# Two more block pairs of the FFN's up-projection in seven half-width products, with the sums of x they need made partly in the projection before

## The chip, the cores and the metric

The program runs on one core of a Trainium2 chip. Its time is device microseconds of one execution, and lower is better. The kernel before took 1469.0 us (median of 3 runs, 1468.36 to 1469.34).

## The reference, cut to what matters

A two-layer encoder on x of 512 tokens by 1024 channels, in float32. Each layer adds three things to x in turn: a mixer (attention in layer 0, an mLSTM in layer 1), a cross-attention to a memory of 256 tokens, and a convolutional feed-forward network (FFN). The last is what the change is about:

```
def conv_ffn(xn, w_up, conv_w, conv_b, w_down):
    h = causal_depthwise_conv(xn @ w_up, conv_w) + conv_b
    g, u = jnp.split(h, 2, axis=-1)
    return (jax.nn.gelu(g) * u) @ w_down
```

`xn` is RMS-normed x, `w_up` is 1024 by 5632, `w_down` 2816 by 1024. The cross-attention ends in a product with `wo` (1024 by 1024) that is added to x.

## The kernel before

x lies transposed in SBUF: eight blocks `x[0..7]` of 128 channels by 512 tokens. Every float32 product is made from two parts of each operand, high and low, in three matmuls (`mm3`, L290 to L292). A weight block is loaded by SP (`raw`), its high part is cast by ScalarE (`wh`), and the low part is subtracted by VectorE (`wl`, L281). So TensorE runs the products, and each operand costs the two other engines a pass.

**Up-projection by pairs.** The FFN (`ffn_steps`, from L1247) makes its 5632 hidden channels in 22 pairs: pair p is block p (gate) and block 22+p (up), 128 channels each. `plain` (from L1431) makes a pair as two blocks of eight k-steps, each step one `mm3` of 512 columns: 48 matmuls. `seven` (from L1451) makes it in Strassen's way (Winograd's form) from seven products of four k-steps with 256 columns: 84 matmuls of half the width. There the two rows of blocks of the weights are A1 and A2, each cut in two halves along k; x is cut in two halves along k and two along tokens (`HALF`). The seven products are p1, p5, p6, p2, p7, p3, p4 in the order in which they run. Products p5, p6, p7 and p4 multiply sums of quarters of x, T1, T3, T2, T4, which don't depend on the pair. These lie as high and low part in `th[k]`, `tl[k]` (k from 0 to 3, 1024 columns each).

**The forms of x.** `forms(k, at)` (L1363 to L1384) makes `th[k]`, `tl[k]`: two scalings on ScalarE into an `hs` tile (L1370), three sums on VectorE into an `sa` tile (L1374, L1381, L1382), a cast on ScalarE (L1383), and a subtraction on VectorE. It takes block k of x for the one half along k and block k+4 for the other. All four forms are made in the FFN, two behind pair 0 and two behind pair 1.

**Which pairs are which.** `SEVEN` names pairs 4 to 21; pairs 0 to 3 are plain.

**Weights of a seven pair.** SP loads both halves of A into `sa` (L1280), then a DMA issued by POOL adds A2 on top of it (`onto`, L1460, with accumulation); SP also loads A1 (`raw`) and half of A2 (`ra`). VectorE makes two more sums (`sb`, L1480, L1486). Then there are five splits into high and low part. Three `sa` tiles, two `sb`, one `ra`, and one each of the small split tiles `s2`, `a22`, `s4`; the wide split tiles `wh`, `wl` have three each and are shared with the plain blocks.

**Between products.** p6 and p7 collect in one PSUM bank, Y. VectorE reads it (`c22`, L1520) before p4 may write it; p3 runs between. VectorE also makes `c12` (L1520) and scales the pair by the norm (L1543). The rest, `tail`, is 4 taps of the convolution on VectorE (L1404), one multiply (L1414), one cast and one subtraction (`al`). Two `hs` tiles hold the unfinished pairs.

**Fill.** From pair 5 on, `fill()` puts blocks of the down-projection (12 matmuls of 512 columns each, `down`) at two places in a pair: between c22 and p3, and behind p4. There are 8 blocks for each group of four activations, so pairs 5 to 16 and 18 have two each, pair 19 has one (ahead of p3), and pairs 4, 17, 20 and 21 none.

**What sets the order.** In the mixers and in the cross-attention a planner, `Plan`, takes the items in the order of their priorities as soon as its own estimate says they are ready; in the FFN another, `Sched`, gives each engine at each step the task that can start first, the one due first among those that can start at once. Each engine then runs its queue in order. A tile that lies where an earlier stage's tile lay waits for that tile's last reader (`reuse_waits="tile"`).

**The stage before the FFN.** `xattn` (L1122) holds its keys in `kth`, `ktl` and its values in `vh`, `vl`, 32 KB a partition in all. Its last part, `p_out` (blocks m = 0 to 7, priorities 100 to 107), is the projection with `wo`: per block 24 matmuls of 512 columns, then on VectorE the sum to x (L618), on ScalarE the scaled high part `xh` (L602), on VectorE the low part `xl` (L603), and the squares for the next norm (L593 to L597). The keys, the values and the scores are done by then.

Of the kernel before, what the change touches and what calls it, by code (L numbers as in the profile page):

```python
# [1 line left out]

# [7 lines left out]
F32 = mybir.dt.float32  # L10
# [15 lines left out]
SEVEN = (4, 5, 6, 7, 8, 9, 10, 11, 12, 13, 14, 15, 16, 17, 18, 19, 20, 21)  # L26
# [209 lines left out]
class Builder:  # L236
# [885 lines left out]
    def xattn(self, layer):  # L1122
        nc, t, tc = self.nc, self.t, self.tc
        with tc.tile_pool(name=f"xa{layer}", bufs=1, reuse_waits="tile") as mp:
            self.mp = mp
            pl = Plan(self.plan, [st["banks"][0] for st in self.fills], s=2, w=2, e=4, q=2, pt=2, wt=3)
            self.pad(mp, 192)
            kth = mp.tile([P, KB8, MEM], F32R, name=f"kth{layer}")
            ktl = mp.tile([P, KB8, MEM], F32R, name=f"ktl{layer}")
            self.pad(mp, 64)  # L1130
            vh = mp.tile([P, 2, DM], F32R, name=f"xvh{layer}")
            vl = mp.tile([P, 2, DM], F32R, name=f"xvl{layer}")
# [4 lines left out]
            for h in range(4):  # L1137
                p = 10 + 10 * h
                ke = []
                for m in (2 * h, 2 * h + 1):  # L1140

                    def keys(ps, m=m, at=0):
                        tmp = self.til(mp, "tmp")
                        nc.vector.tensor_tensor(out=tmp[:, :MEM], in0=ps[:, at : at + MEM], in1=self.memrb, op=ALU.mult)
                        self.split(kth[:, m, :], ktl[:, m, :], tmp[:, :MEM])
# [32 lines left out]
                if h % 2 == 0:  # L1178
                    cs = slice(256 * h, 256 * h + 512)

                    def values(tk, ps, cs=cs):
                        self.evac_tok(ps, self.memr[:, tk : tk + 1], vh[:, tk, cs], vl[:, tk, cs])

                    ve = self.p_proj_tok(pl, t["xv"][layer, h // 2], self.mems, 2, values, prio=p)
# [8 lines left out]
                for i in range(4):  # L1193
# [3 lines left out]
                    def score(h=h, qs=qs, res=res, sl=sl):  # L1197
                        sp = self.bank("s")
                        for d in range(2):
                            kb = 2 * h + d  # L1200
                            self.mm3(sp[:, :MEM], qs[d][0][:, sl], qs[d][1][:, sl], kth[:, kb, :], ktl[:, kb, :], d == 0, d == 1)
# [22 lines left out]
                for d in range(2):  # L1224

                    def weigh(h=h, d=d, pts=pts):
                        c = slice(256 * h + P * d, 256 * h + P * d + P)
                        ps = self.bank("w")
                        for j in range(2):
                            self.mm3(ps[:], vh[:, j, c], vl[:, j, c], pts["h"][:, j, :], pts["l"][:, j, :], j == 0, j == 1)  # L1230
# [7 lines left out]
            self.p_out(pl, t["xo"][layer], lambda: (mh, ml), kd, "ffn", layer, None, 100)  # L1238
            pl.run()
            self.plan = pl  # L1240

# [5 lines left out]
    def ffn_steps(self, layer, mp):  # L1247
# [78 lines left out]
        own = lambda k: (self.xh[k][:], self.xl[k][:])  # L1326
# [23 lines left out]
        th, tl = ([mp.tile([P, 1024], F32R, name=f"t{i}{layer}{k}", tag=f"t{i}{k}") for k in range(4)] for i in "hl")  # L1350
# [12 lines left out]
        def forms(k, at):  # L1363

            st = {}

            def scaled(j):
                if j == 0:
                    st["t"] = hs2[st["_hs"]][:, :, 2:514]
                nc.scalar.activation(st["t"][:, j, :512], self.x[k + 4 * j][:], AF.Identity, scale=self.col("ffn", layer * 8 + k + 4 * j))  # L1370

            def first():
                st["r"] = raw_tile(st, "sa")[:]
                tt_(out=pair(st["r"][:, :512]), in0=pair(st["t"][:, 0, :512]), in1=st["t"][:, :, 256:512], op=ALU.subtract)  # L1374

            T1, T3, T2, T4 = (slice(256 * i, 256 * i + 256) for i in range(4))
            tt_ = nc.vector.tensor_tensor
            a = add("ACT", ACV, lambda: scaled(0), (), at, [("hs", st)])
            a = add("ACT", ACV, lambda: scaled(1), [a], at)
            a = add("DVE", tt(512), first, [a], at, [("sa", st)])  # L1380
            a = add("DVE", tt(256), lambda: tt_(out=st["r"][:, T2], in0=st["t"][:, 1, 256:512], in1=st["r"][:, T1], op=ALU.add), [a], at)  # L1381
            a = add("DVE", tt(256), lambda: tt_(out=st["r"][:, T4], in0=st["t"][:, 1, 0:256], in1=st["r"][:, T2], op=ALU.subtract), [a], at, (), [("hs", st)])  # L1382
            h = add("ACT", act(1024), lambda: nc.scalar.copy(th[k][:], st["r"]), [a], at)  # L1383
            formed.append(add("DVE", tt(1024), lambda: self.sub(tl[k][:], st["r"], th[k][:]), [h], at, (), [("sa", st)]))  # L1384
# [66 lines left out]
        def seven(p, fill):  # L1451
# [46 lines left out]
            X = lambda h, l: (lambda k: (self.xh, self.xl)[0][k + 4 * h][:, HALF[l]], lambda k: self.xl[k + 4 * h][:, HALF[l]])  # L1498
# [75 lines left out]
        for p in range(22):  # L1574
# [5 lines left out]
            if p < 2:  # L1580
                for k in (2 * p, 2 * p + 1):
                    forms(k, clock[0] + 4.0 * (k % 2))
# [247 lines left out]
    def finish(self, mp, ah, al):  # L1830
# [7 lines left out]
        outs = [self.til(mp, f"t{i}{k}", (P, 1024), F32R, bufs=1).bitcast(F32)[:, :512] for k in range(4) for i in "hl"]  # L1838
# [64 lines left out]
    def run(self):  # L1903
        tc = self.tc
        M = bass.MemoryType.PSUM
        with (
# [10 lines left out]
            for layer in range(2):  # L1917
                with tc.tile_pool(name=f"mem{layer}", bufs=1, reuse_waits="tile") as self.memp:
                    (self.mix0, self.mix1)[layer]()
                    self.xattn(layer)  # L1920
                self.ffn(layer)


def col_blocks(w):

    k, m = w.shape
    return w.reshape(k // P, P, m // P, P).transpose(2, 1, 0, 3).reshape(m // P, P, k)

# [16 lines left out]
def layout(i):  # L1945
# [23 lines left out]
    a["up"] = np.stack([col_blocks(i["ffn_w_up"][n]) for n in range(2)])  # L1969
# [40 lines left out]
```

## Time and profile before

| | |
|---|---|
| time, median of 3 | 1469.0 us |
| profiled execution: time, span | 1469.97 us, 1467.1 us |
| TensorE busy | 1452.4 us |
| VectorE busy | 1200.9 us |
| ScalarE busy | 873.7 us |
| output projection of the cross-attention, layers 0 and 1 | about 376 to 407.7 us, about 1084.5 to 1116.2 us |
| pairs 0 to 3 | 407.7 to 451.9 us, 1116.2 to 1160.4 us |

The span runs from the first to the last instruction of the profiled execution; the 2.9 us of its time beside the span are start and end. In the trace's lines a group is named by line, engine, operation and tiles: `acc<-xh,wh` is a matmul into a bank of tile `acc` from `xh` and `wh`. Two numbers ahead of a line of the timeline are its start and its duration in us. Matmuls overlap, so the distance of their starts is their price, and not their duration. Brackets hold the idle time of the engine just before and what ended it. A line of the table by stretches gives for each engine the busy time and the count, then the granted clock, the share of the DMA engines' time and GB/s. A line of the waits gives who waited for whom, the total, the times and the longest.

### The profile page before, as it was taken

The numbers are of one execution on the slowest core, as the hardware profiler recorded it, in microseconds if no ns is written. First come the engines' busy times: TensorE is split into PE (matmuls) and PEld (weight loads), VectorE is DVE, ScalarE is ACT, GpSimd is POOL, SyncE is SP. The second block draws the span as 40 slices with busy tenths as digits, with TensorE's granted clock in tenths as the row PEclk, the third lists the DMA queues.
The fourth block names the chain that finished last, engine by engine and source line by source line (L and its number), as shares of the span: only waits on it lengthen the run. The fifth ranks groups of instructions, "written<-read, shape, count | busy, mean of one in ns | idle before, by whom it ended". The sixth has DMA issues, their size and how long they took to land.

```text
span 1467.1 us, 22604 instructions
## 1 busy us (share of the span) xinstructions
PE 1452.4 (99%) x8503; PEld 1267.8 (86%) x8503; DVE 1200.9 (82%) x2136; ACT 873.7 (60%) x1533; POOL 63.3 (4%) x102
## 2 busy tenths in 40 slices
PE   9999999999999999999999999999999999999998
PEld 7888787888889999999888888888888899999987
DVE  7789985766589999999769988677557999999974
ACT  7688664544476656666457655454445766656654
POOL 0001120000001000000000100000000000000000
PEclk9999999999999999999999999999999999999999
DMA  5222333323238665652223332332323766656322
GB/s 198 87 73 73 122 117 121 115 87 114 86 130 205 168 160 158 154 159 80 85 99 109 115 101 74 121 102 100 115 87 115 187 173 165 158 160 156 109 68 77
DMA packets 64797, 179.14 MB, mean 122 GB/s; under 512 B 7072, under 2 KB 7072, under 8 KB 64688
## 3 DMA queue, kind: packets, MB, share of 16 engines
q1 hardware_dynamic: 58496, 157.71, 32.9%
q0 software_dynamic: 5184, 18.88, 7.6%
q8 instruction: 66, 1.08, 0.3%
q10 hardware_dynamic: 1008, 1.12, 0.2%
q14 instruction: 43, 0.35, 0.1%
HBM read 175.55 MB, written 2.13 MB: 121 GB/s over the span
## 4 chain that ended last, share of the span: by engine, by line
PE 80%; DVE 13%; ACT 3%; issue 2%; DMA 1%; POOL 0%; SPq 0%; ACTq 0%; DVEq 0%; POOLq 0%
PE acc L290 16%; PE acc L291 16%; PE acc L292 15%; PE w L291 5%; PE w L290 5%; PE w L292 5%; DVE wl L281 3%; PE s L290 2%; PE s L292 2%; PE s L291 2%; PE acc L351 2%; DVE c L1404 2%; PE acc L353 2%; PE acc L352 2%; DVE x L770 1%
## 5 line engine op out<-in xcount | busy, mean ns | idle before, releaser
L290 PE MATMUL acc<-xh,wh 128*128 128x512 f32 (+1 forms) x800 | 282.0, 352 | 0.1
L292 PE MATMUL acc<-xh,wl 128*128 128x512 f32 (+1 forms) x800 | 279.9, 350 | 0.2 <-DVE wl L281 0.2
L291 PE MATMUL acc<-xl,wh 128*128 128x512 f32 (+1 forms) x800 | 279.5, 349 | 0.0
L281 DVE TENSOR_TENSOR wl<-raw,wh 128x1024 fp32r<-128x1024 f32 (+4 forms) x199 | 235.7, 1186 | 27.2 <-ACT wh L284 22.8
L284 ACT CAST wh<-raw 128x1024 fp32r<-128x1024 f32 (+1 forms) x135 | 139.3, 1036 | 144.5 <-PE acc L291 88.7
L292 PEld LDWEIGHTS acc<-xh,wl 128*128 128x128 f32 x800 | 150.2, 188 | 20.8 <-DVE wl L281 0.6
L290 PEld LDWEIGHTS acc<-xh,wh 128*128 128x128 f32 x800 | 150.3, 188 | 20.4 <-ACT v L1639 0.6
L291 PEld LDWEIGHTS acc<-xl,wh 128*128 128x128 f32 x800 | 150.3, 188 | 19.9
L1404 DVE SCALAR_TENSOR_TENSOR c<-hs,vec,c 128x512 f32<-128x512 f32 x176 | 128.0, 745 | 7.6 <-ACT c L1397 6.5
L292 PE MATMUL w<-ah,wl 128*128 128x512 f32 x304 | 118.9, 391 | 0.0
L291 PE MATMUL w<-al,wh 128*128 128x512 f32 x304 | 118.5, 390 | 0.0
L290 PE MATMUL w<-ah,wh 128*128 128x512 f32 x304 | 118.4, 390 | 0.0
L1397 ACT ACTIVATE c<-hs,vec 128x512 f32<-128x512 f32 x88 | 70.7, 814 | 46.1 <-DVE hs L1543 38.0
L618 DVE TENSOR_TENSOR x<-w,x 128x512 f32<-128x512 f32 x72 | 49.5, 687 | 22.0 <-PE w L292 22.0
L292 PEld LDWEIGHTS w<-ah,wl 128*128 128x128 f32 x304 | 57.0, 188 | 12.1
L290 PEld LDWEIGHTS w<-ah,wh 128*128 128x128 f32 x304 | 57.1, 188 | 10.0
L291 PEld LDWEIGHTS w<-al,wh 128*128 128x128 f32 x304 | 57.1, 188 | 9.9
L618 DVE TENSOR_TENSOR x<-acc,x 128x512 f32<-128x512 f32 x32 | 22.0, 691 | 49.2 <-PE acc L292 49.2
L290 PE MATMUL acc<-mem,wh 128*128 128x256 f32 (+1 forms) x192 | 61.1, 318 | 0.0
L291 PE MATMUL acc<-mem,wh 128*128 128x256 f32 (+1 forms) x192 | 60.9, 317 | 0.0
L292 PE MATMUL acc<-mem,wl 128*128 128x256 f32 (+1 forms) x192 | 60.7, 316 | 0.0
L1474 ACT CAST wh<-sa 128x1024 fp32r<-128x1024 f32 x36 | 37.8, 1050 | 34.1 <-PE w L291 32.1
(470 smaller groups left out, 3985.0 us busy)
## 6 DMA issues: line engine op xcount, KB each, us to landing
raw<-in_up_dram SPq DMA_DIRECT2D x52, 512.0 KB, 3.3
sa<-in_up_dram SPq DMA_DIRECT2D x36, 512.0 KB, 3.8
sa<-in_up_dram POOLq DMA_DIRECT2D x36, 512.0 KB, 6.2
dr<-in_down_dram SPq DMA_DIRECT2D x64, 256.0 KB, 2.8
ra<-in_up_dram SPq DMA_DIRECT2D x36, 256.0 KB, 2.6
raw<-in_xk_dram SPq DMA_DIRECT2D x16, 512.0 KB, 3.4
raw<-in_wo_dram SPq DMA_DIRECT2D x16, 512.0 KB, 3.4
raw<-in_xq_dram SPq DMA_DIRECT2D x16, 512.0 KB, 3.3
```

The source lines that it names most:

```text
L281: self.nc.vector.tensor_tensor(out=lo, in0=v, in1=hi.bitcast(F32), op=ALU.subtract)
L284: self.nc.scalar.copy(hi, v)
L290: mm(out, wh, xh, start=first, stop=False, skip_group_check=parts)
L291: mm(out, wh, xl, start=False, stop=False, skip_group_check=parts)
L292: mm(out, wl, xh, start=False, stop=last, skip_group_check=parts)
L351: mm(ps, xh[k][:, ts], wh[:, ws], start=(k == 0), stop=False)
L352: mm(ps, xh[k][:, ts], wl[:, ws], start=False, stop=False)
L353: mm(ps, xl[k][:, ts], wh[:, ws], start=False, stop=(k == 7))
L618: self.nc.vector.tensor_tensor(out=self.x[m][:], in0=ps[:], in1=self.x[m][:], op=ALU.add)
L1397: nc.scalar.activation(st["c_"][:, j, :], hs()[:, j, 2:514], AF.Identity, scale=self.col("cw", (layer * 3 + 2) * 44 + blk), bias=self.col( ...
L1404: nc.vector.scalar_tensor_tensor(out=c, in0=hs()[:, j, n : n + 512], scalar=w, in1=c, op0=ALU.mult, op1=ALU.add)
L1474: nc.scalar.copy(s["wh"][:, :cols], raw())
```

## The change

- `SEVEN` takes in pairs 2 and 3, so that pairs 2 to 21 are made by seven products and only pairs 0 and 1 are plain.
- The halves along k are now the even and the odd blocks of x in place of the first four and the last four, so form k takes x[2k] and x[2k+1]. The columns of the up weights are put in that order ahead of the launch (`even_odd`), and plain pairs run their k-steps in the order x0, x2, x4, x6, x1, x3, x5, x7.
- Forms 0, 1 and 2 are made in `xattn`, inside the output projection: form k at priority 100+2k+2, after all attention is weighed and after `xprep` of block 2k+1. They use the tiles `pth` and `ptl` of the attention as working space. Form 3 is made in the FFN, behind pair 0 (`forms(3, ...)`).
- `th[k]`, `tl[k]` are tiles `kv0` to `kv7` of a new pool `keys` at the other end of SBUF, opened ahead of the cross-attention and closed after the FFN. The same eight tiles hold the keys and values before that. With it the other tiles of `xattn` and of the FFN move to lower addresses.

```
-SEVEN = (4, 5, 6, 7, 8, 9, 10, 11, 12, 13, 14, 15, 16, 17, 18, 19, 20, 21)
+SEVEN = (2, 3, 4, 5, 6, 7, 8, 9, 10, 11, 12, 13, 14, 15, 16, 17, 18, 19, 20, 21)
...
+            kv = [self.til(self.kp, f"kv{i}", (P, 1024), F32R, bufs=1) for i in range(8)]
+            self.pad(self.kp, 128)
+            kth, ktl = ([v[:].rearrange("p (a b) -> p a b", b=MEM) for v in vs] for vs in (kv[:2], kv[2:4]))
+            vh, vl = kv[4:6], kv[6:]
...
             self.p_out(pl, t["xo"][layer], lambda: (mh, ml), kd, "ffn", layer, None, 100)
+            self.forms = []
+            used = [d for k in kd for d in kd[k]]
+
+            def form(k):
+                th, tl = (self.til(self.kp, f"kv{i + k}", (P, 1024), F32R, bufs=1) for i in (0, 4))
+                self.forms.append((th, tl))
+                if k == 3:
+                    return
+                f, r = self.til(mp, "pth", (P, 2, 512)), self.til(mp, "ptl", (P, 1024))
+                for fn in self.form_steps(k, layer, f, r, th, tl):
+                    fn[1]()
+
+            for k in range(4):
+                pl.add(
+                    lambda k=k: form(k), 0, [*used, *self.xdone[2 * k + 1]], 100 + 2 * k + 2, order=[last_form] if k else [],
+                    chain=(("A", 1.5), ("D", 1.4), ("A", 1.0), ("D", 1.2)) if k < 3 else (),
+                )
+                last_form = pl.items[-1]
...
+        return [
+            ("A", lambda: gained(0)),
+            ("A", lambda: gained(1)),
+            ("D", lambda: tt_(out=pair(r[:, :512]), in0=pair(t[:, 0, :]), in1=t[:, :, 256:512], op=ALU.subtract)),
+            ("D", lambda: tt_(out=r[:, T2], in0=t[:, 1, 256:512], in1=r[:, T1], op=ALU.add)),
+            ("D", lambda: tt_(out=r[:, T4], in0=t[:, 1, 0:256], in1=r[:, T2], op=ALU.subtract)),
+            ("A", lambda: nc.scalar.copy(th[:], r[:])),
+            ("D", lambda: self.sub(tl[:], r[:], th[:])),
+        ]
...
-        own = lambda k: (self.xh[k][:], self.xl[k][:])
+        blk = lambda k: 2 * (k % 4) + k // 4
+        own = lambda k: (self.xh[blk(k)][:], self.xl[blk(k)][:])
...
-        th, tl = ([mp.tile([P, 1024], F32R, name=f"t{i}{layer}{k}", tag=f"t{i}{k}") for k in range(4)] for i in "hl")
+        th, tl = zip(*self.forms)
...
-            if p < 2:
-                for k in (2 * p, 2 * p + 1):
-                    forms(k, clock[0] + 4.0 * (k % 2))
+            if p == 0:
+                forms(3, clock[0])
...
+                        self.kp = keys.enter_context(tc.tile_pool(name=f"keys{layer}", bufs=1, side="right", reuse_waits="tile"))
```

More of the change, by code (lines that the diff above doesn't have):

```diff
@@ L1 @@
 import math
+from contextlib import ExitStack
 import numpy as np
@@ L1917, in run @@
             for layer in range(2):
[L1918 to L1921, printed above, removed]
+                with ExitStack() as keys:
+                    with tc.tile_pool(name=f"mem{layer}", bufs=1, reuse_waits="tile") as self.memp:
+                        (self.mix0, self.mix1)[layer]()
+                        self.kp = keys.enter_context(tc.tile_pool(name=f"keys{layer}", bufs=1, side="right", reuse_waits="tile"))
+                        self.xattn(layer)
+                    self.ffn(layer)
 def col_blocks(w):
```

61 lines of the change are left out of this document (36 added, 25 removed).

## The prediction

> **What bounds the kernel now.** I read the page first, then the waits of TensorE, then the timeline for the price of one matmul, then the busy time by stretches.
>
> ```profile
> span 1467.1 us, 22604 instructions
> PE 1452.4 (99%) x8503; PEld 1267.8 (86%) x8503; DVE 1200.9 (82%) x2136; ACT 873.7 (60%) x1533; POOL 63.3 (4%) x102
> PE 80%; DVE 13%; ACT 3%; issue 2%; DMA 1%; POOL 0%; SPq 0%; ACTq 0%; DVEq 0%; POOLq 0%
> ```
>
> TensorE is busy 99% of the span and carries 80% of the chain that ended last, so the time falls by what its stream of matmuls gets shorter, as long as nothing new holds it up. What a matmul costs is the distance of starts:
>
> ```profile
> 441.72 0.39 PE L290 MATMUL acc<-xh,wh 128*128 128x512 f32 x1
> ...
> 444.44 0.39 PE L290 MATMUL acc<-xh,wh 128*128 128x512 f32 x1
> ...
> 453.30 0.28 PE L290 MATMUL s<-th,wh 128*128 128x256 f32 x1
> ...
> 458.74 0.28 PE L290 MATMUL s<-xh,s4h 128*128 128x256 f32 x1
> ```
>
> In a plain pair 12 matmuls of 512 columns take 444.44 - 441.72 = 2.72 us, 0.2267 each. In pair 4 (seven products) 48 of 256 columns take 458.74 - 453.30 = 5.44 us, 0.1133 each: exactly half, so seven products lose nothing by narrowness. The only repeated wait of TensorE in the FFN is this:
>
> ```profile
> PE acc L290 <- DVE hs L1520: 2.5, 6, 0.5
> ```
> ```profile
> 460.89 0.28 PE L291 MATMUL acc<-xl,wh 128*128 128x256 f32 x1
> 461.01 0.41 DVE L1520 TENSOR_TENSOR hs<-acc,u 128x256 f32<-128x256 f32 x1
> 461.48 0.38 PE L290 MATMUL acc<-th,a22h 128*128 128x256 f32 x1 [0.31 <-DVE hs L1520]
> 461.70 0.28 PE L291 MATMUL acc<-tl,a22h 128*128 128x256 f32 x1
> ```
>
> That is p4 waiting for VectorE to read Y (c22). p7 was through at 458.74, c22 came 2.3 us later, and p3 and most of the next pair's p1 covered all but the end. The price is more than the 0.31 shown: 460.89 to 461.48 is 0.59 where 0.11 is usual, and the next step is 0.22, so 0.59 us in all. VectorE is late because in the FFN's opening it is full:
>
> ```profile
> 376.00:407.70 31.70, 31.70 (x141) 26.27 (x140) 21.31 (x27) 15.16 (x22) 0.10 (x1) 1.00 0.36 120
> 407.70:430.10 22.40, 22.40 (x99) 18.21 (x98) 19.12 (x27) 15.98 (x22) 0.00 (x0) 1.00 0.38 124
> 430.10:451.90 21.80, 21.80 (x97) 18.05 (x97) 21.80 (x34) 15.70 (x21) 1.86 (x2) 1.00 0.67 182
> 451.90:463.30 11.40, 11.09 (x97) 10.86 (x96) 11.40 (x18) 7.93 (x15) 1.71 (x2) 1.00 0.83 195
> 523.00:538.00 15.00, 15.00 (x110) 14.02 (x110) 14.04 (x23) 9.08 (x17) 0.85 (x1) 1.00 0.61 158
> ```
>
> These are the output projection, pairs 0 and 1, pairs 2 and 3, pair 4, and a stretch of filled pairs. VectorE (fourth number) has 10.4 us free in the projection, 3.3 in pairs 0 and 1, nothing until pair 4 is through, and 1 us in 15 later. The granted clock is 1.00 throughout.
>
> **The change, part by part.** *Seven products for pairs 2 and 3.* A plain pair is 48 x 0.2267 = 10.88 us of TensorE, a pair of seven 84 x 0.1133 = 9.52. Saved: 1.36 a pair, four pairs in two layers, **5.44 us**. The Trainium skill (TensorE: Matmul & The Clock Gate, section "Wait — 56ns, not 53.3ns?") has a fixed 2.5 ns on each matmul beside its columns; by that, an estimate, 84 narrow matmuls for 48 wide ones would save 1.18 a pair and 4.7 in all. The rows, with exactly half, don't show such a term, and I keep 5.44.
>
> *VectorE's load in the opening.* Its prices, again from starts:
>
> ```profile
> 422.93 1.29 DVE L1441 TENSOR_TENSOR hs<-acc,rb 128x512 f32<-128x512 f32 x2
> ...
> 443.61 0.68 DVE L1441 TENSOR_TENSOR hs<-acc,rb 128x512 f32<-128x512 f32 x1
> 444.21 0.41 DVE L1382 TENSOR_TENSOR sa<-hs,sa 128x256 f32<-128x256 f32 x1
> 444.55 0.74 DVE L1404 SCALAR_TENSOR_TENSOR c<-hs,vec,c 128x512 f32<-128x512 f32 x1
> 445.21 1.22 DVE L281 TENSOR_TENSOR wl<-raw,wh 128x1024 fp32r<-128x1024 f32 x1
> 446.34 1.22 DVE L281 TENSOR_TENSOR tl<-sa,th 128x1024 fp32r<-128x1024 f32 x1
> ```
>
> From 443.61 on: 512 columns 0.60, 256 columns 0.34, a tap 0.66, 1024 columns 1.13. A plain pair: two splits 2.26, two evictions 1.20, four taps 2.64, multiply and `al` 1.20; sum 7.30. A pair of seven: three passes of 1024 (two splits, the scaling) 3.39, seven of 512 (two sums, three splits, multiply, `al`) 4.20, c22 and c12 0.68, taps 2.64; sum 10.91. So two pairs add 2 x 3.61 = 7.2 us a layer. Three forms moved out take away 3 x (0.60 + 0.34 + 0.34 + 1.13) = 7.2. VectorE's work up to the end of pair 4 stays 19.12 + 21.80 + 11.40 = 52.3 us, while TensorE's stretch, now 55.6 us, shrinks by 2.72 to 52.9. It fits, with 0.6 us to spare, if the 3.3 us free in pairs 0 and 1 can be used. I take it that most can. The gaps lie in the chain of the norm, ahead of 422.93, the first row above, when evictions and taps first have something to do; three forms gone from there leave the sums and splits of pair 2 as the work at hand, if its weights have come.
>
> *Pair 2's weights.* They are wanted 22 us earlier than any seven pair's today.
>
> ```profile
> sa<-in_up_dram SPq DMA_DIRECT2D x36, 512.0 KB, 3.8
> sa<-in_up_dram POOLq DMA_DIRECT2D x36, 512.0 KB, 6.2
> ```
> ```profile
> 404.97 1.04 SPq L1280 DMA_DIRECT2D ra<-in_up_dram  x1
> ...
> 435.42 5.37 SPq L1280 DMA_DIRECT2D sa<-in_up_dram  x2
> ```
>
> The first load into the FFN's own tiles starts at 404.97, as the attention's `mixed` tiles get free, and `sa` will lie over the same tiles. Today `sa` waits until 435 only because the forms turn through its three buffers. With one form left: 405 + 3.8 + 6.2 = 415, then a cast and a split, about 2.2 with hand-overs: 417. p5, the first to use it, comes at 430.1 + 1.4 = 431.5, and the wide split tile it goes into gets free at about 424.7, when the third of the four plain blocks is through (430.1 less 5.44). So 6 us in hand; the four added pairs' accumulating DMAs cost nothing on the path.
>
> *The forms in the output projection.* Here every block of the projection shows gaps:
>
> ```profile
> 402.26 1.05 ACT L1294 CAST wh<-raw 128x1024 fp32r<-128x1024 f32 x1 [3.24 <-PE acc L291]
> 403.22 0.72 ACT L602 ACTIVATE xh<-x,vec 128x512 fp32r<-128x512 f32 x1
> 403.84 0.62 ACT L596 ACTIVATE sqt<-x 128x512 f32<-128x512 f32 x1
> ```
> ```profile
> 402.48 0.69 DVE L618 TENSOR_TENSOR x<-acc,x 128x512 f32<-128x512 f32 x1 [2.09 <-PE acc L292]
> ...
> 404.48 0.75 DVE L603 SCALAR_TENSOR_TENSOR xl<-x,vec,xh 128x512 fp32r<-128x512 f32 x1
> ```
>
> A form is on ScalarE 2 x 0.62 + 0.96 = 2.2 us, on VectorE 2.41. Three make 6.6 and 7.2 us, where 16.5 and 10.4 are free. The chain itself (scalings, sums, cast, subtraction) takes 1.24 + 1.28 + 0.96 + 1.13 = 4.6 us, and in order: the cast waits on ScalarE for the sums, the subtraction on VectorE for the cast. Behind them queue the sum to x, the next scaled block, and a weight's cast. Each may come 1 to 3 us later. Nobody on TensorE feels it: the cast at 402.26 waited for the end of a block on TensorE and serves the block two later, so it has about 10 us, and four banks take the projection's sums. x6 is now used fourth in the first FFN block, at 407.7 + 3 x 0.68 = 409.8, where its low part (404.48) is through at 405.2: 4.5 us in hand. I cost this at nothing; without that cover it would be one chain less the gap, 4.6 - 2.1 = 2.5 us for the last form of a layer.
>
> *The pool on the other side.* The first writer of a key tile now waits for the last readers of the mixer's tiles at the top of SBUF. Today:
>
> ```profile
> 969.64 0.69 DVE L618 TENSOR_TENSOR x<-acc,x 128x512 f32<-128x512 f32 x1 [2.09 <-PE acc L292]
> 970.25 0.75 DVE L1144 TENSOR_TENSOR tmp<-acc,memrb 128x256 f32<-128x256 f32 x2
> ```
>
> The keys come only behind the mixer's last sum to x, when its last product is through, so the wait is over by then. Nothing. Form 3's turn through the two `hs` tiles gives pair 1 the tile of pair 0; its eviction moves some 2 us back, and its bank isn't asked for until pair 3. Nothing.
>
> *New waits of p4.* Pairs 2 and 3 have no fill, like 4, 17, 20 and 21. Those eight (two layers) show six waits of 2.5 us in all; with 0.28 of restart each (0.59 - 0.31) that is 4.2 us, 0.52 a pair. Four new ones: **+2.1 us**. From below nothing, since VectorE may be on time in pair 2; from above 0.5 + 0.28 = 0.78 each, 3.1. I take 2.1, which the same kind of pair shows.
>
> **Sum.** -5.4 + 2.1 = -3.3 us. The profiled execution took 1469.97, 0.97 over the median, and I take the difference off the median: 1469.0 - 3.3 = **1465.7 us**.
>
> **The rivals.**
>
> - *No new wait.* VectorE does c22 at once, as the forms are gone. For it: by my sum it is level with TensorE. Against it: six of eight such pairs wait. 1469.0 - 5.4 = 1463.6.
> - *VectorE sets the opening.* If the 3.3 us stay idle, because the norm's chain leaves only gaps shorter than a pass or the weights come late, its work and gaps fill the same 55.6 us, and TensorE is held back to it in pairs 3 and 4 by c22 and the `hs` tiles. The 2.7 us a layer are eaten: 1469.0. For it: 100% of VectorE from 430 to 463. Against it: the taps may lag by more than half a pair before a tile is missed.
> - *Slower: the accumulating DMA of pair 2 is late.* Place: SP's queue, then POOL's. Should `sa` be queued behind a load that waits for the `raw` tile of pair 2 itself (free only when its splits are made, about 425), it lands at 425 + 10 + 2.2 = 437, 5.7 us behind p5, in each layer: 1469.0 - 5.4 + 11.4 + 2.1 = 1477. It decides from an issue of `sa` later than 431.5 - 12.2 = 419. For it: POOL's transfer takes 6.2 where SP's takes 3.8. Against it: the load has 14 us until then. The Trainium skill (SBUF — State Buffer, section "SBUF: two separate sides") says that a DMA issued by GpSimd can starve for descriptors while VectorE works in a two-port mode, which would lengthen this very transfer. The trace can't tell that from the adding itself; it shows 6.2 against 3.8 and no more.
> - *Not what it says.* The products move, but the projection loses what they gain, the 2.5 us above once a layer: 1469.0 - 3.3 + 5 = 1470.7.
>
> **How the numbers follow.** Forecast 0.50, no new wait 0.15, VectorE's opening 0.20, late DMA 0.10, projection 0.05. The forecast's own range is 1463.6 + 0.8 to 1463.6 + 3.1 and a little, 1464.4 to 1467.2. The range reaches over the first two rivals, 1463.3 to 1469.3, and leaves out the late DMA and the projection. About 0.2%, 2.9 us, is what a measurement can tell from no change here: faster than 1466.1 is the first rival and some two thirds of the forecast, 0.50; within it the rest of the forecast, VectorE's opening and the projection, 0.40; slower 0.10.
>
> **What would show it.** `acc<-xh,wh` of 512 columns falls by 64 matmuls in each of the three groups, `acc<-th,a22h` rises from 144 to 160. In layer 0 the first 256-column product starts near 430.1 and not 451.9, and layer 0's FFN ends 1.5 to 2.7 us earlier. The wait of p4 for c22 is listed some nine times, near 3.8 us. The projection's row keeps TensorE at 31.70 of 31.70, with VectorE near 28.5. VectorE in pairs 0 and 1 is nearly full. I am wrong if TensorE waits in pairs 2 to 5 for `sa`, `wl` or `hs`, or if its busy time in the projection breaks.

## The result, and the profile after

The kernel became slower, not faster: 1474.4 us (median of 6 runs, 1473.1 to 1478.0) against 1469.2 us (6 runs of before, 1468.4 to 1470.5). The ratio is 1.004, 95% interval 1.003 to 1.0051. The forecast was 1465.7, with a range to 1469.3. The profiled execution of after is the longest of its six, 1478.04 us with a span of 1476.3. In the second experiment one of five executions took 1596.5 us at a mean granted clock of 0.85; it is left out of the median given here, and counted in the 1478.1 us that the eighth experiment's expectation names.

The line numbers of the changed kernel are not those of before: `mm3` is L291 to L293, the low parts L282, the accumulating DMA L1503, pair sums L1523 and L1529, the casts of a seven pair L1517, c22 and c12 L1563.

From the page of the changed kernel, its busy times by engine and the chain that ended last:

```profile
PE 1454.4 (99%) x8647; PEld 1275.6 (86%) x8647; DVE 1215.2 (82%) x2160; ACT 885.2 (60%) x1565; POOL 65.4 (4%) x106
PE 81%; DVE 9%; ACT 4%; DMA 3%; issue 2%; SPq 0%; POOL 0%; ACTq 0%; DVEq 0%; POOLq 0%
```

TensorE has 144 matmuls more, as planned (4 x 36), and its busy time rose by 2 us where it should have fallen by 5.4. That is a first sign of slower matmuls; the rows below show them. The share of DMA in the chain rose from 1% to 3%. Who kept TensorE waiting, from the waits of after (total, times, longest):

```profile
PE s L293 <- DVE wl L282: 4.7, 2, 3.2
PE acc L291 <- DVE hs L1563: 2.7, 6, 0.6
PE s L291 <- ACT wh L1517: 0.8, 1, 0.8
```

The first and the third are new; they are waits of p5 for the split of pair 2's `sa`. The wait of p4 for c22, of which I had forecast four more, is listed six times, as before, and none of the six is in pair 2 or 3: their p4 starts without a listed wait in both layers (449.15 and 457.31 in FFN 0). Now the stretches of the prediction, busy time by engine, clock and DMA share in the changed kernel:

```profile
376.00:407.70 31.70, 31.70 (x142) 26.25 (x141) 28.65 (x39) 21.75 (x30) 0.21 (x2) 1.00 0.34 111
407.70:430.10 22.40, 22.40 (x100) 18.17 (x98) 14.57 (x22) 10.97 (x16) 2.71 (x3) 1.00 0.78 220
430.10:451.90 21.80, 17.76 (x123) 16.88 (x122) 20.04 (x31) 14.45 (x24) 0.86 (x1) 0.84 0.62 145
```

The projection took the forms in without a gap: TensorE 31.70 of 31.70, VectorE 28.65 as forecast. In pairs 0 and 1 VectorE did 14.57 us, less than the 19.12 of before, though work waited for it; the DMA share went from 0.38 to 0.78. In the next stretch TensorE lost 4 us, and its clock fell to 0.84 of full.

Where VectorE's time went is in its timeline in the changed kernel:

```profile
418.81 0.69 DVE L525 SCALAR_TENSOR_TENSOR sq<-sqt,sq 128x512 f32<-128x512 f32 x1 [0.79 <-ACT sqt L522]
425.43 0.69 DVE L1523 TENSOR_TENSOR sb<-sa,raw 128x512 f32<-128x512 f32 x1 [5.93 <-DMA sa<-in_up_dram]
...
427.18 0.68 DVE L519 TENSOR_TENSOR sqt<-sqt,rb 128x512 f32<-128x512 f32 x1
...
428.38 0.68 DVE L531 SCALAR_TENSOR_TENSOR rb<-sqt,sq 128x512 f32<-128x512 f32 x1
...
435.23 1.22 DVE L282 TENSOR_TENSOR wl<-sa,wh 128x1024 fp32r<-128x1024 f32 x1
```

The last step of the norm in the kernel before:

```profile
422.20 0.69 DVE L530 SCALAR_TENSOR_TENSOR rb<-sqt,sq 128x512 f32<-128x512 f32 x1
```

L525, L519 and L531 are three of the last steps of the norm. Between them now stands L1523, pair 2's first sum, which reads the `sa` that a DMA accumulates. VectorE took its queue in order: it stood still for 5.93 us with the norm unfinished, though ScalarE's part of it (L528) was through at 421.0. L530 ended the norm at 422.9 before; the same step, now L531, ends at 429.1. All that needs the norm, the evictions of pairs 0 and 1, their taps and what queues behind, came more than 6 us later, the split of pair 2's `sa` among it, at 435.23. It was wanted from 431.9 on, when p5 should have begun, as TensorE's timeline shows in the changed kernel:

```profile
431.75 0.28 PE L293 MATMUL acc<-xh,wl 128*128 128x256 f32 x1
432.81 0.38 PE L291 MATMUL s<-kv,wh 128*128 128x256 f32 x1 [0.78 <-ACT wh L1517]
433.03 0.28 PE L292 MATMUL s<-kv,wh 128*128 128x256 f32 x1
436.50 0.58 PE L293 MATMUL s<-kv,wl 128*128 128x256 f32 x1 [3.19 <-DVE wl L282]
436.88 0.41 PE L291 MATMUL s<-kv,wh 128*128 128x256 f32 x1
```

The last two rows lie 0.38 apart where two neighbours lie 0.11 apart: after the wait the matmuls are slow. Busy time and clock in steps of 2 us say why (the third number from the right is the granted clock), changed kernel:

```profile
434.00:436.00 2.00, 0.00 (x0) 0.00 (x0) 2.00 (x4) 1.62 (x3) 0.00 (x0) 0.96 0.78 211
436.00:438.00 2.00, 1.50 (x7) 1.50 (x8) 2.00 (x4) 0.89 (x2) 0.00 (x0) 0.50 0.26 23
440.00:442.00 2.00, 2.00 (x12) 2.00 (x10) 1.84 (x3) 0.82 (x2) 0.86 (x1) 0.50 0.00 0
```

The wait itself cost 4.3 us (starts 0.95 and 3.36 late), and then the clock was halved for some 6 us, which cost 3 us more.

Why `sa` was late: the loads on SP's queue and the accumulating DMA on POOL's in the changed kernel, with the time of issue first:

```profile
410.16 0.33 SPq L1324 DMA_DIRECT2D raw<-in_up_dram  x1
410.53 0.95 SPq L1324 DMA_DIRECT2D sa<-in_up_dram  x2
```
```profile
416.52 1.00 POOL L1503 DMA_DIRECT2D sa<-in_up_dram  x1 [13.11 <-DMA sa<-in_up_dram]
```

A weight load that waited for its `raw` tile until 410.16 stood in front of `sa`. So `sa` left at 410.53, not at 405; its two transfers took 6.0 and 8.9 us where the prediction had 3.8 and 6.2, with the DMA engines 0.7 to 1.0 busy from 408 to 426 us. The sum in the queue waited for the second to land, at 425.4.

The account by stretches, from the profiled executions. FFN 0 and 1 run from the last sum to x in the projection to the wait of p4 of 0.44 us that all kernels show late in the FFN; after has them at 408.05 and 658.34, 1122.79 and 1368.50.

| us | before | after | difference |
|---|---|---|---|
| up to FFN 0 | 407.92 | 408.05 | +0.1 |
| FFN 0 | 243.98 | 250.29 | +6.3 |
| between | 464.52 | 464.45 | -0.1 |
| FFN 1 | 244.12 | 245.71 | +1.6 |
| the rest | 106.56 | 107.80 | +1.2 |

So the loss is in the two FFNs. (This execution lost 9.2 us of span; the medians differ by 5.2.) In FFN 1 VectorE waited 3.0 us at the same place, for the other operand of the sum, and TensorE 2.1, without a fall of the clock. The 1.2 at the end lie behind TensorE's last instruction, where the writes of the output landed later; the first and the eighth experiment, which have the same products in that place, don't show it.

### The profile page after: what moved, and what is told of

The parts are those of the page before. It is cut to its first block, busy times and chain, and to the rows that moved or that the text cites. A ratio compares the mean times of both kernels' runs of the same rounds, so it can differ in the third digit from the quotient of the medians.

```text
span 1476.3 us, 22994 instructions
## 1 busy us (share of the span) xinstructions
PE 1454.4 (99%) x8647; PEld 1275.6 (86%) x8647; DVE 1215.2 (82%) x2160; ACT 885.2 (60%) x1565; POOL 65.4 (4%) x106
## 4 chain that ended last, share of the span: by engine, by line
PE 81%; DVE 9%; ACT 4%; DMA 3%; issue 2%; SPq 0%; POOL 0%; ACTq 0%; DVEq 0%; POOLq 0%
PE acc L291 16%; PE acc L292 16%; PE acc L293 16%; PE w L292 5%; PE w L293 5%; PE w L291 5%; PE s L293 3%; PE s L292 3%; PE s L291 3%; PE acc L352 2%; DVE wl L282 2%; PE acc L354 2%; PE acc L353 2%; DMA sa<-in_up_dram 2%; DVE c L1447 1%
## 5 line engine op out<-in xcount | busy, mean ns | idle before, releaser
L291 PE MATMUL acc<-xh,wh 128*128 128x512 f32 (+1 forms) x768 | 266.6, 347 | 0.1
L293 PE MATMUL acc<-xh,wl 128*128 128x512 f32 (+1 forms) x768 | 264.3, 344 | 0.7 <-DVE wl L282 0.6
L292 PE MATMUL acc<-xl,wh 128*128 128x512 f32 (+1 forms) x768 | 264.0, 344 | 0.0
L282 DVE TENSOR_TENSOR wl<-raw,wh 128x1024 fp32r<-128x1024 f32 (+3 forms) x195 | 231.2, 1186 | 24.6 <-ACT wh L285 22.5
L293 PEld LDWEIGHTS acc<-xh,wl 128*128 128x128 f32 x768 | 144.6, 188 | 19.1 <-DVE wl L282 1.3
L291 PEld LDWEIGHTS acc<-xh,wh 128*128 128x128 f32 x768 | 144.8, 189 | 18.2 <-ACT v L1681 0.6
L292 PEld LDWEIGHTS acc<-xl,wh 128*128 128x128 f32 x768 | 144.7, 188 | 17.4
L293 PE MATMUL w<-ah,wl 128*128 128x512 f32 x304 | 119.0, 391 | 0.0
L291 PE MATMUL w<-ah,wh 128*128 128x512 f32 x304 | 118.4, 390 | 0.0
L293 PEld LDWEIGHTS w<-ah,wl 128*128 128x128 f32 x304 | 57.1, 188 | 12.0
L291 PEld LDWEIGHTS w<-ah,wh 128*128 128x128 f32 x304 | 57.1, 188 | 10.0
L1517 ACT CAST wh<-sa 128x1024 fp32r<-128x1024 f32 x40 | 42.1, 1052 | 32.9 <-PE w L292 30.1
L291 PE MATMUL acc<-mem,wh 128*128 128x256 f32 (+1 forms) x192 | 61.1, 318 | 0.0
L293 PE MATMUL acc<-mem,wl 128*128 128x256 f32 (+1 forms) x192 | 60.7, 316 | 0.0
L1503 POOL DMA_DIRECT2D sa<-in_up_dram x40 | 34.4, 861 | 482.2 <-DVE x L619 115.9
```

Source lines behind the costliest of these rows:

```text
L282: self.nc.vector.tensor_tensor(out=lo, in0=v, in1=hi.bitcast(F32), op=ALU.subtract)
L291: mm(out, wh, xh, start=first, stop=False, skip_group_check=parts)
L292: mm(out, wh, xl, start=False, stop=False, skip_group_check=parts)
L293: mm(out, wl, xh, start=False, stop=last, skip_group_check=parts)
L1503: return add("POOL", 0.0029 * cols, lambda: nc.gpsimd.dma_start(out(), src(), accum_op=ALU.add), deps, due, (), (), 6.0)
L1517: nc.scalar.copy(s["wh"][:, :cols], raw())
```

## The experiments

**Theory A**: the order of VectorE's queue is at fault. Sums of seven pairs that wait for their accumulating DMA stand ahead of work that TensorE needs sooner. **Rival B**: the opening holds too much VectorE work, whatever its order. **Rival C**: the moved forms or the new place of their tiles cost the time. **Rival D**: the DMA engines are full, so the weights are late wherever the sums stand. Each kernel starts from the changed one; its ratio is against runs of before on the same chip (medians of before 1469.0 to 1469.1).

### Undo the products, keep the forms (C)

```
-SEVEN = (2, 3, 4, 5, 6, ...
+SEVEN = (4, 5, 6, ...
```

> Forms made in the output projection and held in the pool on the other side, as in the changed kernel, but pairs 2 and 3 stay plain, so TensorE has the products of the kernel before. Theory A (VectorE's queue holds pair 2's first sum, which waits for its accumulating DMA, ahead of the norm's last steps): no such sum stands there any more, the time is that of before or a little below, 1467 to 1470 us. Rival C (the moved forms or the new place in SBUF cost the time by themselves): 1472 us or more, of the 5.2 + 5.4 us lost against the plan the larger part stays. Rival B (the opening holds too much VectorE work): two plain pairs need 48 x 0.227 us each and their weights come ready split into two parts, so VectorE is freed: about 1469 us as well.

Measured: 1467.4 us, ratio 0.999 (0.9981 to 0.9998). C falls: the forms in the projection and the new pool cost nothing, they gain 1.7 us. FFN 0 took 243.41, FFN 1 243.48, each 0.6 less than before.

### Undo half of the products

```
-SEVEN = (2, 3, 4, 5, 6, ...
+SEVEN = (3, 4, 5, 6, ...
```

> Pair 2 plain, pair 3 by seven products: half of the change's product saving (2 pairs of 1.36 us = 2.7 us over both layers) and the first accumulating DMA is due one plain pair (10.9 us) later. Theory A: the sum waits for nothing or stands behind the norm in VectorE's queue; 1469.2 - 2.7 = 1466.5 us, at most 1.5 us of waits more. Rival B (VectorE's sum of work in the opening): about half of the overload stays, so some 4 of the 11.4 us excess of waits and 1470 to 1472 us. Rival C: 1471 us or more.

Measured: 1477.6 us (median of four), ratio 1.0057 (1.0043 to 1.0071). One pair less by seven products, and slower than the changed kernel by 3.2: a miss for A and B as I had put them. Only C's "1471 us or more" covers it, and C fell with the first experiment. VectorE and then TensorE in this kernel:

```profile
422.26 0.69 DVE L1523 TENSOR_TENSOR sb<-sa,raw 128x512 f32<-128x512 f32 x1 [3.34 <-DMA sa<-in_up_dram]
```
```profile
444.58 0.38 PE L291 MATMUL acc<-xh,wh 128*128 128x256 f32 x1 [0.97 <-ACT wh L1517]
446.67 0.58 PE L291 MATMUL acc<-kv,s2h 128*128 128x256 f32 x1 [1.71 <-ACT acc L1556]
```

I had thought that 10.9 us more of time would put pair 3's sum behind the norm. It stands ahead of it here as well, although nobody needs it before 442. VectorE waits 3.34 us, and the delay runs down the queues until TensorE waits for ScalarE, which waits for VectorE's evictions. Then the clock is halved, in both layers here, which costs 2.8 us each. So the mechanism is A's; what was wrong was my guess of the order.

### Put the norm ahead of pair 2's sum

```
             def s2_():
-                tt_(out=raw_tile(sb, "sb")[:], ...
+                to = raw_tile(sb, "sb")
+                if p == 2:
+                    nc.vector.tensor_copy(to[:, :8], self.rb[:, :8])
+                tt_(out=to[:], ...
```

The planner had emitted the sum behind the norm all along; the built program has it in front, and a new dependency in the planner alone left the queue as it was. A small copy that reads the norm's result and writes into the sum's tile is a dependency of data, and it moves the sum. So what sets VectorE's order is the built program, and not the planners alone as the description of the kernel before has it.

> The changed kernel with one VectorE copy of 8 columns of the norm's result into the sum's tile ahead of pair 2's first sum, so that this sum cannot stand ahead of the norm's last three steps; loads, DMAs and products unchanged. Theory A: VectorE's idle 5.9 us at 419.5 to 425.4 in FFN 0 falls below 2 us, the norm ends at about 423 us instead of 429, most of the 8.0 and 3.4 us of late starts on TensorE go: 1465 to 1469 us. Rival B: VectorE has the same work plus 0.1 us, so nothing changes: 1473 to 1476 us. A third reading, D (pair 2's weights are late by themselves, whatever stands in front): the norm is early, but pair 2's products still wait some 4 us for the split of sa in FFN 0: 1469 to 1473 us.

Measured: 1474.0 us, ratio 1.0032 (1.0021 to 1.0044): no gain, a miss for A and by its number a point for B. VectorE in this kernel (the sums are L1526):

```profile
421.95 0.69 DVE L531 SCALAR_TENSOR_TENSOR rb<-sqt,sq 128x512 f32<-128x512 f32 x1
...
423.88 0.16 DVE L1525 COPY sb<-rb 128x8 f32<-128x8 f32 x1
426.57 0.69 DVE L1526 TENSOR_TENSOR sb<-sa,raw 128x512 f32<-128x512 f32 x1 [2.53 <-DMA sa<-in_up_dram]
```

The norm is early, as meant. But the sum that comes next is pair 3's (pair 2's follows at 427.84), and it waits for its own accumulating DMA, issued at 417.26 and landed 9.3 us later, with the taps and pair 2's splits behind it. TensorE waits 2.29 us in FFN 0 and 2.73 in FFN 1. This gave no verdict yet between A with more sums, B and D.

### Load `sa` earlier

```
-            b1 = load(sa, "sa", up2[p][:, :, :512], 1024, at - 20.0)
+            b1 = load(sa, "sa", up2[p][:, :, :512], 1024, at - 20.0, "POOL" if p in (2, 3) else "SP")
```

> The changed kernel, the loads of sa for pairs 2 and 3 issued on POOL's queue instead of SP's, where they stood behind a weight load that waited for its slot until 410.2 us; VectorE's work unchanged. Theory A: sa starts when its space is free, about 405 us, lands some 5 us earlier, VectorE waits under 1.5 us and the time is 1465 to 1469 us. Rival B: 1473 to 1476 us. Rival D (the DMA engines are full between 405 and 425 us, so an earlier issue only makes other loads late): sa still lands after 422 us or the plain pairs' weights come late, 1471 to 1476 us.

Measured: 1481.8 us, ratio 1.009 (1.0076 to 1.0104), the slowest of all and above all three ranges. `sa` came early: pair 2's sum ran at 418.85, pair 3's at 421.39. Then the next sum, pair 4's, stood in the queue, VectorE in this kernel:

```profile
431.42 0.69 DVE L1523 TENSOR_TENSOR sb<-sa,raw 128x512 f32<-128x512 f32 x1 [4.60 <-issue]
432.03 1.22 DVE L282 TENSOR_TENSOR wl<-sa,wh 128x1024 fp32r<-128x1024 f32 x1
```

The profile names no releaser. But pair 4's accumulating DMA was issued at 424.41 and took 6.9 us, so it landed at about 431.3. Behind it waited the split of pair 2's `sa`, whose data had long been there. An earlier transfer doesn't help if the order lets the next late one take its place.

### Hold back the sums of pairs 2 to 5 (A against B)

As in the third, and pairs 3, 4 and 5 behind the split of the pair before (`prev` is its wide split `f1`):

```
+                if p in (3, 4, 5):
+                    nc.vector.tensor_copy(to[:, :8], prev[1]["wl"][:, :8])
```

> The changed kernel with the first sums of pairs 2 to 5 held back in VectorE's queue by copies of 8 columns: pair 2's behind the norm, those of pairs 3, 4 and 5 behind the split of the pair before (so that no sum that waits for its accumulating DMA stands in front of work that TensorE needs sooner). Loads and DMAs as in the changed kernel. Theory A (in-order VectorE queue held by sums whose DMA lands late): VectorE idles under 1.5 us between 418 and 445, the split of pair 2's sa is done by 431.5, TensorE's waits at 430 to 450 fall under 1 us, 1464 to 1467 us. Rival B (VectorE has too much work in the opening): idle goes, yet the split is still 2 us or more late, TensorE waits 2 to 3 us per layer and its clock drops as in the third experiment: 1471 to 1475 us.

Measured: 1468.0 us, ratio 0.9988 (0.9979 to 0.9997): 6.4 us below the changed kernel, with the same products, loads and DMAs. The copies are meant to move four sums, and the built order of what stands around them moves too, so the queue as a whole is what changed. VectorE in this kernel (the sums are L1530):

```profile
422.24 0.69 DVE L531 SCALAR_TENSOR_TENSOR rb<-sqt,sq 128x512 f32<-128x512 f32 x1
422.97 1.29 DVE L1484 TENSOR_TENSOR hs<-acc,rb 128x512 f32<-128x512 f32 x2
424.17 0.16 DVE L1527 COPY sb<-rb 128x8 f32<-128x8 f32 x1
424.37 0.69 DVE L1530 TENSOR_TENSOR sb<-sa,raw 128x512 f32<-128x512 f32 x1
...
430.03 1.22 DVE L282 TENSOR_TENSOR wl<-sa,wh 128x1024 fp32r<-128x1024 f32 x1
```

No wait at all, and the split of `sa` is through at 431.2, in time. The stretch of pairs 2 and 3 in this kernel, to set against the 17.76 and 0.84 above:

```profile
430.10:451.90 21.80, 21.70 (x184) 21.41 (x183) 21.77 (x35) 16.35 (x30) 1.71 (x2) 1.00 0.74 198
```

A holds, and B falls as the cause of the loss: VectorE has the same work and the copies besides (1215.3 us busy, against 1215.2). D falls too: the loads stand where they stood and are in time. Pair 2's accumulating DMA landed at 422.7 here, 2.8 us earlier than in the changed kernel, but it landed at the same time in the third experiment and gained nothing there. What is missing is the gain: A expected 1464 to 1467.

### Both (order and early load)

The edits of the fourth and the fifth together.

> As the fifth experiment, and the loads of sa of pairs 2 and 3 on POOL's queue, from 405 us on. Theory A: pair 2's sum runs as soon as the norm and the first evictions are done, without a wait, 1463.5 to 1466 us, 0.5 to 1.5 us below the fifth. Rival B: 1471 to 1475 us as without it. Rival D (crowded DMA engines): what sa gains, a plain pair's weights or the third pair's sa lose, 1468 us or more.

Measured: 1467.8 us, ratio 0.999 (0.9982 to 0.9999), as without the early load: above A's range. With the right order the 405 instead of 410.5 buys nothing on balance. The two FFNs took 243.29 and 243.22 us, together 0.9 us more than in the fifth. A new wait of TensorE for the norm's operand costs 1.5 us of them; it stands in the two kernels with the moved loads and in no other. Without it the early loads would have brought some 0.7 us, less than it costs.

### Leave the accumulating DMAs of pairs 2 and 3 out

```
+            if p not in (2, 3):
                 b1 = onto(lambda: sa["sa"][:], lambda: A2, 1024, [b1], at - 16.0)
```

> The changed kernel without the two accumulating DMAs of pairs 2 and 3 in each layer: their sa holds one block instead of the sum of two, so this part of the computation is left out. VectorE's work is the same. Theory A: sa is there when its first load has landed (about 415 us), VectorE's sums wait little, 1464 to 1468 us. Rival B: the same VectorE work in the same stretch, 1472 to 1475 us.

Measured: 1475.0 us, ratio 1.0042 (1.0029 to 1.0054). By its number this is a miss for A and a point for B. VectorE in this kernel says otherwise:

```profile
429.50 0.69 DVE L1524 TENSOR_TENSOR sb<-sa,raw 128x512 f32<-128x512 f32 x1 [3.85 <-DMA sa<-in_up_dram]
```

That is pair 4's sum, which had moved up when the two before it no longer waited, as in the fourth. Leaving a late transfer out let the next one block.

### The second again, with the order mended

`SEVEN` from 3; pair 3's sum behind the norm, those of pairs 4 to 6 behind the split of the pair before.

> The second experiment (pair 2 plain, seven products from pair 3) with the sums held back as in the fifth: pair 3's behind the norm, those of pairs 4 to 6 behind the split of the pair before. Theory A (sums that wait for accumulating DMAs in front of other VectorE work): the 2.1 us gap and the clock drop of the second experiment go in both layers, 1478.1 falls to 1465.5 to 1468 us. Rival B (too much VectorE work): less is to be done in the opening than in the fifth, but the second experiment was slow for the same reason, so it stays above 1472 us.

Measured: 1467.7 us, ratio 0.9992 (0.9983 to 1.0001), against 1477.6 without the copies: 9.9 us by the order of a few instructions. That is in A's range; B had said that it stays above 1472.

### Only the later sums held back

The fifth without its copy for pair 2.

> The counterpart of the third experiment: pair 2's sum stands ahead of the norm's last steps as in the changed kernel, only the sums of pairs 3, 4 and 5 are held back. Theory A: VectorE's 5.9 us wait at 419.5 to 425.4 stays and with it late evictions and a late split of pair 2's sa, TensorE waits 1 to 3 us per layer: 1470 to 1474 us, between the fifth (1468.0) and the changed kernel (1474.4). If pair 2's place alone were to blame, it would be 1474 us; if only the later sums were, 1468 us.

Measured: 1475.1 us, ratio 1.0045 (1.0032 to 1.0058), 1.1 us above A's range. The wait of VectorE is 3.99 us and not 5.9, since the accumulating DMA landed at 423.4. VectorE and TensorE in this kernel (the sum is L1528):

```profile
423.38 0.69 DVE L1528 TENSOR_TENSOR sb<-sa,raw 128x512 f32<-128x512 f32 x1 [3.99 <-DMA sa<-in_up_dram]
```
```profile
433.85 0.39 PE L293 MATMUL s<-kv,wl 128*128 128x256 f32 x1 [1.91 <-DVE wl L282]
```

With the third this makes a square: pair 2's sum held back 1474.0, the later ones held back 1475.1, both 1468.0, none 1474.4. Either sum in front is enough to lose everything, so undoing one alone shows nothing, and I would have dropped A after the third experiment had I stopped there.

### Less VectorE work in the mended order (B, weaker form)

The fifth, with nothing done in the taps of pairs 0 and 1:

```
             def tap(j, n):
+                if p < 2:
+                    return
```

> The fifth experiment without the eight convolution taps of pairs 0 and 1 on VectorE in each layer (this part of the computation is left out), 8 x 0.66 = 5.3 us less VectorE work per opening. Theory A: in the fifth TensorE no longer waits for VectorE, so little changes, 1467 to 1468.5 us. Rival B, weaker form (VectorE at its limit still costs the fifth the 2 us per layer that it misses against the plan): 1463.5 to 1465 us.

Measured: 1467.3 us, ratio 0.9988 (0.9979 to 0.9997); 0.7 us below the fifth for 10.6 us of VectorE work less over two layers. That is A's range, so B doesn't explain the missing gain either. The first FFN took 242.65 (the fifth 242.91).

### How long a wait halves the clock

A kernel of its own: runs of 300 products of 256 columns, with waits between them made by chains of VectorE operations.

> Only TensorE products of 256 columns in runs of 300, between them waits made by chains of VectorE operations on 8 or 256 columns, from about 0.6 us to about 8 us, each length once or twice in mixed order; nothing of the reference is computed. If the granted clock falls after a wait of some length, the starts after it lie 0.2 us apart instead of 0.113: expected after waits of 3 us and more and not after those of 2 us and less, for some 8 us each. If waits are not the cause, all starts stay at 0.113 us. Time about 650 us.

Rows of TensorE (start, length of a run of 300, the wait ahead of it in brackets):

```profile
82.34 36.25 PE L81 MATMUL ps<-xh,wh 128*128 128x256 f32 x300 [2.48 <-DVE xh L90]
...
397.00 38.69 PE L81 MATMUL ps<-xh,wh 128*128 128x256 f32 x300 [5.44 <-DVE xh L90]
437.51 36.26 PE L81 MATMUL ps<-xh,wh 128*128 128x256 f32 x300 [1.83 <-DVE xh L90]
...
520.66 37.74 PE L81 MATMUL ps<-xh,wh 128*128 128x256 f32 x300 [2.16 <-DVE xh L90]
561.22 36.25 PE L81 MATMUL ps<-xh,wh 128*128 128x256 f32 x300 [2.81 <-DVE xh L90]
599.96 37.74 PE L81 MATMUL ps<-xh,wh 128*128 128x256 f32 x300 [2.48 <-DVE xh L90]
```

A run is 36.26 us undisturbed and up to 38.7 with a halved clock. Waits of 0.26 to 1.83 us, six of them, never halved it; waits of 3.80 to 6.75, four of them, always did; of six between 2.16 and 3.14 three did, and the same 2.48 did once and not the other time. One, the first of 3.14 us, went against my line of 3 us, and the four between 2 and 3 us fell both ways, so there is no sharp length. The execution took 688 us, where I had expected 650, since the starts lie 0.120 apart here. A fall cost 1.3 to 2.4 us, so the halved stretch was about twice that, 2.7 to 4.9 us, and not the 8 that I had put.

## Why the prediction was wrong

**The step that failed** is *Pair 2's weights*: "So 6 us in hand; the four added pairs' accumulating DMAs cost nothing on the path." I followed the data (load, accumulation, cast, split) to the product that needs it, and did not ask where in VectorE's queue the instruction stands that waits for it, and what is queued behind. In the fifth experiment the sum runs at 424.4 and is in time; in the changed kernel it stood at 419.5, ahead of the norm. The transfer landed at 425.4, not at 415. With 2.2 us for cast and split that would still have been in time for p5, but it was 5.9 us too late for the queue. (The margin was mis-added as well: a wide tile that is free at 424.7 and 2.2 us of cast and split leave 4.6 us before 431.5, not 6.) The fifth and the eighth experiment show it: with the order of VectorE's queue changed, and the same products and loads, 6.4 and 9.9 us come back.

- *Seven products for pairs 2 and 3, -5.44*: the matmul counts are as put, and narrow matmuls start at 0.113 where nothing disturbs them. But only part of it arrived in any version. From the first experiment to the fifth, which differ in these products and the copies, FFN 0 fell by 0.50 and FFN 1 by 0.73: 1.2 of 5.4.
- *New waits of p4, +2.1*: none of the four came. In the changed kernel and in the fifth, p4 of pairs 2 and 3 starts without a listed wait. Yet 4.2 us didn't arrive, and TensorE's rows show where. I added up how far each start between 430 and 520 us lies behind its place at 0.2267 and 0.1133 us a matmul. In the fifth that is 1.4 us in single late starts and 1.5 in a slightly slower pace, told below; in the first experiment it is 0.3 and 0.35. The difference of 2.2 is what FFN 0 misses (2.72 less 0.50), and FFN 1 comes to 2.0 in the same way (2.72 less 0.73). In the tenth there is no slow pace, but the late starts are 2.2: 0.52 at 434.4 (a wait for a low part), 1.10 at 460 (c22 of pair 4), 0.29 at 462.8 and 0.34 at 494. So the sum needed a term of about 2 us a layer, and what I had put in its place was another wait and half the size.
- *VectorE's load in the opening*: the sum was right, and that it fits, if the gaps can be used. They can, in the order of the fifth, where VectorE worked 19.52 us in pairs 0 and 1 and 21.77 in the next stretch. The condition "if its weights have come" was the weak place, and I costed it by the data and not by the queue.
- *Issue of `sa` at 405*: it was 410.53, behind a load waiting for a `raw` tile. The kernel before had the same load on SP's queue at 410.04, between the two rows that I showed, so its trace could have told me. I had named that queue in the rival. Harmless by itself: early loads changed nothing on balance in the sixth.
- *The forms in the output projection, nothing* and *the pool on the other side, nothing*: no cost; the first experiment even gains 1.7 us, which I hadn't forecast.
- *The rivals*: the slower one, at 0.10, had the right place (SP's queue, then POOL's) and the right sign, at 1477. Its deciding point was wrong. I let it decide from an issue at 419, by the need of p5; it decides by the need of the norm, and VectorE was free for the sum at 419.5, 10 us before the landing that I had allowed (431.5 - 2.2). The Trainium skill's rule on starved descriptors (SBUF — State Buffer, "SBUF: two separate sides") can't be told apart from plain crowding here: pair 2's accumulating transfer took 8.9 us in the changed kernel with the DMA engines 0.7 to 1.0 busy, and pair 3's still took 9.7 in the fifth, where nothing urgent stood behind it.
- *What my account left out altogether* is that a wait of TensorE costs more than itself: 4.3 us of waiting in FFN 0 brought 3 us of half clock.

The 9.0 us by which FFN 0 misses its plan of -2.7 are then 4.3 of waits, 3 of the halved clock, and 1.7 that the fifth experiment misses as well. (Against the first experiment, whose FFNs are 0.6 us shorter than before's, the fifth misses 2.2.) What stays open is what sets the slower pace and the single late starts, and the later landing of the output in some of the kernels.

## What to carry to other kernels

A wait must be placed in the queue of its engine before it is priced: an instruction that waits for a late transfer delays everything behind it, however early its own result comes. If the planner's order isn't the order of the built program, a small copy that carries a real dependency sets it; and where several instructions can take the blocking place, hold them all back, since mending one alone shows nothing. Of the kernels here none gains more than about 0.1% on before (forms alone 1467.4, fifth 1468.0, sixth 1467.8), so the change is worth its simplest part at most.

## What the runs showed of the hardware

**Waits of 2 to 3 us halve the clock in some cases and not in others.** The third experiment waited 2.29 us in FFN 0 and kept its clock, waited 2.73 in FFN 1 and lost it (busy time of TensorE and granted clock in that kernel):

```profile
1142.00:1144.00 2.00, 0.08 (x1) 0.79 0.63 199
1144.00:1146.00 2.00, 2.00 (x9) 0.50 0.30 94
1148.00:1150.00 2.00, 2.00 (x11) 0.50 0.00 0
1150.00:1152.00 2.00, 2.00 (x19) 1.00 0.91 121
```

It cost 3.0 us. Short waits that follow each other closely can do it too: in the second experiment 0.97 and 1.71 us with one recorded matmul between them were enough, while the six short waits of the last experiment had 300 products between them. It may also be why the runs spread: the six of the changed kernel had a mean clock of 0.997 to 0.999 and 1478.0 to 1473.1 us, where kernels without long waits stay within 2.6 us; the fourth, with long waits and a spread of 0.9, is an exception. The Trainium skill (TensorE: Matmul & The Clock Gate, "Part 1: The HAM clock gate (the "warmup" mystery)") has it that the clock falls to half after an idle window of about 3.4 us, of a monitor whose windows run freely. The free-running window fits what the rows show, the same 2.48 us with both outcomes; the length doesn't: falls came after waits of 2.16 and 2.48 us.

**Narrow products have a second, slightly slower pace at full clock.** TensorE in the fifth experiment, and the same products in the tenth:

```profile
447.45 0.28 PE L291 MATMUL s<-xh,s4h 128*128 128x256 f32 x1
...
450.28 0.28 PE L291 MATMUL acc<-kv,a22h 128*128 128x256 f32 x1
```
```profile
447.41 0.28 PE L291 MATMUL s<-xh,s4h 128*128 128x256 f32 x1
...
450.13 0.28 PE L291 MATMUL acc<-kv,a22h 128*128 128x256 f32 x1
```

From the first to the second row are 24 matmuls: 2.83 us (0.118 each) in the one and 2.72 (0.113) in the other, both with a granted clock of 1.00. The slow pace lasted from 435.6 to 460 in the fifth, which cost some 0.9 us. It shows in FFN 1 of the changed kernel too, and from 465 to 471 in the kernel before. It began behind a late start in all three; but in the tenth a late start at 434.4 was followed by the usual pace. What sets and ends it wasn't tried.
